# Turning the compressed queries and the softmax sums on VectorE instead of TensorE, in a hybrid encoder layer on one Trainium2 core

## The chip, the cores and the metric

The kernel runs on one core of one Trainium2 chip. Its engines work from queues of their own, each in its own order: TensorE (PE in the profile; PEld is its weight load), VectorE (DVE), ScalarE (ACT), GpSimd (POOL) and SyncE (SP), which does no arithmetic here and issues nearly all DMAs. An engine waits on semaphores that other engines or landed DMAs raise; while the instruction at the head of a queue waits, everything behind it in that queue waits too. The metric is the device time of one execution in microseconds (us); lower is better.

## The reference, cut to what matters

One layer projects x (2048 x 1024) into two groups of heads, runs gated linear attention (GLA) on the one and latent attention (MLA) on the other, and projects their concatenated outputs back, with a residual and a LayerNorm. All of it is float32. What the change touches is in the MLA branch (the compressed queries `c_q`, 256 wide, and the sums of the softmax) and in the final LayerNorm's reciprocal square root:

```python
def mla_branch(c_q, c_kv, k_rope, gate, positions, q_norm_g, w_uq, kv_norm_g, w_ukv):
    q = (rms_norm(c_q, q_norm_g) @ w_uq).reshape(B, S, MLA_HEADS, MLA_D_NOPE + MLA_D_ROPE)
    ...
    def attend(blk):
        qn, qr = blk
        s = (jnp.einsum('bqhd,bkhd->bhqk', qn, k_nope, preferred_element_type=jnp.float32)
             + jnp.einsum('bqhr,bkr->bhqk', qr, k_r, preferred_element_type=jnp.float32))
        p = jax.nn.softmax(s, axis=-1)
        return jnp.einsum('bhqk,bkhv->bqhv', p.astype(v.dtype), v)
    ...
    return o * jax.nn.silu(gate)

# at the end of the layer
x = layer_norm(DEEPNORM_ALPHA * x + mixed, ln_g[layer], ln_b[layer])
```

## The kernel before

Matrix products keep float32 accuracy by splitting each operand into a high part (`hi`, a rounding copy, on ScalarE unless said otherwise) and a low part (`lo`, operand minus high part, on VectorE or GpSimd) and multiplying three times. The sequence is cut into 16 chunks of 128 positions. There are four stages.

- **First sweep** (`sweep_a`, up to about 340 us): backward over the chunks, the GLA projections and the backward state.
- **Second sweep** (`sweep_c`, about 345 to 580 us): forward over the chunks, two chunks a step, eight steps (0 to 7). Chunk c is number j = c % 2 of its step. Per chunk: the projection `ipm`; its norms; the compressed queries `cq`; their transposition `cqT_h`, `cqT_l` (128 features on the partitions, two halves); the products `pqr` (rotary queries, from the transposed `cqT`) and, once per step for both chunks, `pq` (absorbed queries). Beside it runs the GLA forward state: DMA `SU` fetches a stored state update, GpSimd adds it to the state (`c_Sf2`, L1484), scales it into `SU` (`c_M`, L1493), and TensorE uses that in `Ob`. VectorE forms `og` and turns it in 32x32 blocks (`oT`); it goes to memory and is loaded back block by block later. The keys take that same way: `kvx`, `skv`, `kv_load`.
- **Attention** (about 600 to 1075 us): 16 blocks of one head by 512 queries. Per block 16 key tiles in eight pairs; scores `pS`, ScalarE copies, VectorE maxima, subtraction, exponential, splitting, product `o`. GpSimd and VectorE add the exponentials up over the key tiles into `acc`; `tsum` turns these 128 x 512 partial sums with four 128x128 transposes on TensorE, VectorE reduces them (`rcp`, L1714) and takes the reciprocal, ScalarE's queue stores it (`keep`).
- **Output projection** with residual and LayerNorm (to the end), whose reciprocal square root is `rsqrt_b` (L437 to L440) on a 128x1 column.

In the second sweep and in attention the order on every engine is a hand-written table: each helper `c_<name>` or step has a place (PLACE_C, PLACE_C_FIRST for step 0, PLACE_C_LAST for step 7, PLACE), in units of steps, or of tile pairs in attention; all are sorted by place, and `in_order` ties each engine to that order. A place sets order alone, not time.

In a step before the change, for each chunk, TensorE turns `cq` with two 128x128 transposes into PSUM (`c_tm`, L1407), ScalarE copies that into the high part (`c_cqTh`), VectorE subtracts for the low part (`c_cqTl`), and TensorE's `pqr` reads both: L418 and L419 the high part, L420 the low one. In TensorE's order `pqr` of a step's second chunk (j = 1) stands in the next step, among its gate products `pz`.

Of the kernel before, what the change touches and what calls it, by code (L numbers as in the profile page):

```python
# [18 lines left out]
P = 128  # L19
# [4 lines left out]
H = 4  # L24
# [68 lines left out]
    rmax=1.27,  # L93
    bmax=1.48,
    tot=11.2,
    tsum=12.04,
    rcp=13.55,
    keep=14.21,
    oh=12.34,
# [34 lines left out]
SETUP_C = ("lset", "u15", "u14", "wS", "wH", "wL", "pb0", "wa0", "wh0", "wl0", "pb1", "wa1", "wh1", "wl1")  # L134
STEP_C = ("gm1", "gm2", "gm3", "gm4", "sgm", "pq", "qah", "qal", "sqa")
CHUNK_C = ("lx", "xh", "xl", "lS", "lq", "lo", "lu", "sqm", "ssm", "rml", "rmd", "cq", "ckv", "krf", "krfa",
    "krsh", "krsl", "vh", "vl", "kvx", "tm", "cqTh", "cqTl", "ckvTh", "ckvTl", "krT", "pqr", "qrf", "qrfa",
    "tq", "qrTh", "qrTl", "Sf1", "Sf2", "M", "Ob", "oib", "sqO",
    "ss", "rgl", "rgd", "og", "oT", "soT")

FETCH_C = ("lx", "xh", "xl")
LAST_C = ("ckvTh", "ckvTl", "krT")
KV_LOADS = tuple((2 * s - 4, 2 * s - 2, float(s)) for s in range(2, NCH // 2)) + ((12, 14, 8.27),)


PLACE_C = dict(
    skv=1.6,
    kvx=(1.12, 1.44),
    ipa=(-0.08, 0.695),
    ipb=(-0.014, 0.701),  # L150
    ipc=(0.026, 0.723),
# [3 lines left out]
    pqr=(0.849, 1.355),  # L155
    tq=(1.13, 1.56),
    xh=(-0.19, -0.054),
    sqO=(0.272, 0.988),
    rgl=(0.283, 1.029),
    sqm=(0.14, 0.858),  # L160
    rml=(0.352, 0.993),
# [132 lines left out]
    sqO=(0.15, 0.435),  # L294
    rgl=(0.229, 0.457),
    sqm=(0.101, 0.657),
    rml=(0.162, 0.878),
    cq=(0.463, 1.041),
    ckv=(0.35, 1.075),
    vh=(0.865, 1.252),  # L300
# [7 lines left out]
    ss=(0.166, 0.454),  # L308
    rgd=(0.332, 0.461),
    og=(0.336, 0.508),  # L310
    ssm=(0.103, 0.733),
    rmd=(0.254, 1.022),
    krf=(0.139, 0.6),
    cqTl=(0.598, 1.211),
    ckvTl=(0.88, 1.703),
# [37 lines left out]
class K:  # L353
# [80 lines left out]

    def rsqrt_b(self, u, y, t, w, r):
        nc = self.nc
        nc.vector.tensor_tensor(t, y, u, ALU.mult)  # L437
        nc.vector.tensor_tensor(w, t, y, ALU.mult)
        nc.vector.tensor_scalar(t, w, -0.5, 1.5, ALU.mult, ALU.add)
        nc.vector.tensor_tensor(r, t, y, ALU.mult)  # L440
        return r
# [58 lines left out]
    def run(self):  # L500
        tc, nc, ins = self.tc, self.nc, self.ins
        with ExitStack() as top:
            cp = top.enter_context(tc.tile_pool(name="const", bufs=1))
            self.cp = cp
            dp = top.enter_context(tc.tile_pool(name="scr", bufs=1, space=DRAM))
            self.qd_s = [dp.tile([P, H * P], F32, name=f"qd_s{c}") for c in range(NCH)]
            self.oi_s = [dp.tile([P, H * P], F32, name=f"oi_s{c}") for c in range(NCH)]
            self.su_s = [dp.tile([P, H * P], F32, name=f"su_s{c}") for c in range(NCH)]
            self.u_s = [dp.tile([P, H * P], F32, name=f"u_s{c}") for c in range(NCH)]
            self.qa_s = [[dp.tile([P, H, QB], F32, name=f"q{p}_s{b}") for p in "hl"] for b in range(NQB)]  # L510
            self.qr_s = [dp.tile([2, QB // P, P, 256], F32, name=f"qr_s{b}") for b in range(NQB)]
# [39 lines left out]
            self.sweep_c()  # L551
            bcs.close()
            psum.close()
            self.wof = top.enter_context(tc.tile_pool(name="wof", bufs=PRE_W, side="right", reuse_waits="tile"))
            self.attention()
# [589 lines left out]
    def sweep_c(self):  # L1145


        with ExitStack() as ctx:
# [8 lines left out]

            def put(n, st, fn, *a, j=None):
                last = st == len(steps) - 1
                p = PLACE_C[n]  # L1160
                p = (last and PLACE_C_LAST.get(n)) or (not st and PLACE_C_FIRST.get(n)) or p
                todo.append((st + (p if j is None else p[j]), len(todo), fn, a))

# [11 lines left out]
            for d in chunks:  # L1175
                for n in range(4):
                    put("ip" + "abcd"[n], d["st"], self.c_ip, d, n, j=d["j"])
                for n in CHUNK_C:
                    late = d["st"] == len(steps) - 1
                    if n in (LAST_C if not late else ("kvx",)):  # L1180
                        continue
                    if (d["st"] or n not in FETCH_C) and (d["c"] < NCH - 1 or n not in ("Sf1", "Sf2")):
                        put(n, d["st"], getattr(self, "c_" + n), d, j=d["j"])
# [46 lines left out]

    def scale_w(self, ct):
        if ct:
            self.wabs = self.w1.tile([P, 2, H, P], F32, tag="qrT", name="wabs", bufs=2)
        wa = self.wabs[:, ct]
        self.nc.vector.scalar_tensor_tensor(wa, self.wa[ct], self.gq[:, ct:ct + 1],
                                            self.gkv_b[:, None, :].to_broadcast([P, H, P]), ALU.mult, ALU.mult)
# [160 lines left out]
    def kv_load(self, cs):  # L1397
        for r, src in self.blocks_of(self.kv_s[cs].rearrange("c i p (m t) -> (c i) p m t", t=32)):
            self.nc.sync.dma_start(self.kvT[r, cs].rearrange("p c i (b t) -> p (c i b) t", t=32).bitcast(F32), src)

    def c_tm(self, d):
        tp = d["tm"] = self.tr.tile([P, 4, P], F32, tag="tr", name=f"tm{d['c']}")
        src = (d["cq"][:, 0:P], d["cq"][:, P:2 * P])
# [3 lines left out]
            self.nc.tensor.transpose(tp[:, i], e, self.ident)  # L1407

    def c_cqTh(self, d):
        s = d["step"]  # L1410
        if "cqT_h" not in s:
            for p in "hl":
                s[f"cqT_{p}"] = self.w1.tile([P, 2, 2, P], F32R, tag=f"cqT_{p}", name=f"cqT_{p}{d['st']}")
        self.hi(s["cqT_h"][:, :, d["j"]], d["tm"][:, 0:2])

    def c_cqTl(self, d):
        s, j = d["step"], d["j"]
# [30 lines left out]
    def c_qrTh(self, d):  # L1448
        s = d["step"]
        if "qrT" not in s:  # L1450
            s["qrT"] = self.w1.tile([P, 2, 2, 256], F32R, tag="qrT", name=f"qrT{d['st']}", bufs=2)
        self.hi(s["qrT"][:, d["j"], 0], d["tq"])

    def c_qrTl(self, d):
# [120 lines left out]
    def attention(self):  # L1575
# [4 lines left out]
        with ExitStack() as ctx:  # L1580
# [117 lines left out]
            def close(i, shape, name, other):  # L1698
# [2 lines left out]
                p, tag = other if i == nb - 1 else (pX, "x")  # L1701
                return p.tile(shape, F32, tag=tag, name=name)

            def tsum(i):
                d = stt[i]
                d["x"] = close(i, [P, 4, P], f"sx{i}", (pA, "ap"))
                for e in range(4):
                    nc.tensor.transpose(d["x"][:, e], d["as"][:, 0, e * P:(e + 1) * P], self.ident)

            def rcp(i):  # L1710

                d = stt[i]
                rc = bs.tile([P, 4], F32, tag="rc", name=f"rc{i}")
                V.tensor_reduce(rc, d["x"], AX.X, ALU.add)  # L1714
                V.reciprocal(rc, rc)
                d["rc"] = rc

            def keep(i):
                h, b = blocks[i]
                Ac.dma_start(self.r_s[b][:, h].rearrange("o (e p) -> p (o e)", p=P), stt[i]["rc"])  # L1720

            def turn(i):

# [55 lines left out]
            put(0.5, nc.sync.dma_start, wv, self.ins["wv"])  # L1779
            put(8.6, wv_hi)  # L1780
            put(9.9, self.lo, wv_l, wv, wv_h, "pool")
            own = (("tot", tot), ("tsum", tsum), ("rcp", rcp), ("keep", keep), ("oh", oh), ("ol", ol), ("y", y), ("yc", yc))
            own_late = tuple(e for e in own if e[1] is not keep)
            for i in range(nb):
                for j in range(NP):
                    t = NP * i + j
# [311 lines left out]
```

## Time and profile before

| what | value |
|---|---|
| median of 3 runs | 1267.62 us (1267.16 to 1270.45) |
| the profiled execution | 1266.33 us; its span, first to last instruction, 1264.5 us |
| busy over the span | PE 98%, PEld 87%, DVE 72%, ACT 57%, POOL 57% |
| second sweep, one step (437.5 to 465.0 us) | PE 27.50 of 27.50 us, DVE 17.52, ACT 13.72, POOL 15.17; DMA engines 81% |
| attention (600 to 1100 us) | PE 498.38 of 500 us, DVE 423.76, ACT 409.81, POOL 446.67 |

A row of a timeline gives start, duration, engine, line of the program, operation, output<-inputs and shape; in square brackets the engine's idle time before it and who ended it. "xN" is a run of N of them merged. SPq, ACTq mark a queue's DMA issue, not the transfer. Starts are counted from the first instruction. Matmul durations overlap: what one costs on PE is the distance between starts. In the groups of one tile or line, three numbers with slashes are the least, the median and the most, in ns, and for "DMA to landing" in us from issue to landing.

### The profile page before, as it was taken

The page shows a single profiled execution, that of the slowest core. Times are in us where ns is not written, and L with a number is a line of the kernel's source. Part 1 is how long each engine was busy: PE and PEld are TensorE (multiplying, and loading weights), DVE is VectorE, ACT ScalarE, POOL GpSimd, SP SyncE. Part 2 cuts the span into 40 slices and gives each one's busy share as a digit, 9 for nine tenths or more (in the row PEclk, how much of TensorE's full clock was granted, in tenths as well). Part 3 has the DMA queues.
Part 4 walks back from the last instruction along what each step waited for, and adds up shares of the span by engine and source line. Part 5 has one row for each costly group of instructions (what it writes and reads, how often), then busy time and mean ns, then how long its engine had stood idle before and what let it go on. Part 6 is the DMA issues. An engine that isn't in the chain of part 4 may idle for free.

```text
span 1264.5 us, 19632 instructions
## 1 busy us (share of the span) xinstructions
PE 1242.3 (98%) x6890; PEld 1094.2 (87%) x6890; DVE 906.0 (72%) x1654; ACT 725.8 (57%) x1149; POOL 721.7 (57%) x443
## 2 busy tenths in 40 slices
PE   8999999999999999999999999999999999999997
PEld 7999999999899999988788888888888888887886
DVE  6635555554565666575988888888888888379998
ACT  7543443444664545445788888788888888411110
POOL 0132323223364555421798888889999999935441
PEclk9999999999999999999999999999999999999999
DMA  8224655556757788868422222202244120477773
GB/s 294 79 81 123 139 143 139 144 135 159 268 179 212 227 244 239 240 183 195 73 37 48 41 43 43 59 9 59 59 94 92 41 43 26 125 205 199 206 199 116
DMA packets 284338, 165.61 MB, mean 131 GB/s; under 512 B 185574, under 2 KB 241774, under 8 KB 284240
## 3 DMA queue, kind: packets, MB, share of 16 engines
q1 hardware_dynamic: 276176, 162.23, 48.2%
q0 software_dynamic: 672, 2.10, 0.4%
q8 instruction: 55, 0.90, 0.4%
q10 hardware_dynamic: 7392, 0.03, 0.3%
q14 instruction: 43, 0.35, 0.1%
HBM read 105.54 MB, written 58.75 MB: 130 GB/s over the span
## 4 chain that ended last, share of the span: by engine, by line
PE 86%; DVE 5%; DMA 3%; issue 2%; SPq 2%; ACT 1%; POOL 1%; DVEq 0%; POOLq 0%; ACTq 0%
PE pz L1266 7%; PE ipm L1335 5%; PE o L418 5%; PE o L419 5%; PE o L420 5%; PE pS L1599 4%; PE pS L1600 4%; PE pS L1602 4%; PE pS L1601 4%; PE pS L1603 4%; PE ipa L418 4%; PE ipa L420 4%; PE ipa L419 4%; PE ipg L420 2%; PE ipg L418 2%; PE ipg L419 2%
## 5 line engine op out<-in xcount | busy, mean ns | idle before, releaser
L370 POOL TENSOR_TENSOR pl<-s,ph 128x1024 fp32r<-128x1024 f32 x128 | 306.6, 2412 | 51.5 <-ACT ph L364 40.9
L1621 DVE TENSOR_TENSOR rm<-pS,rm 128x512 f32<-128x512 f32 x210 | 144.8, 690 | 36.3 <-ACT s L1608 30.7
L1608 ACT ACTIVATE s<-pS 128x1024 f32<-128x1024 f32 x128 | 131.3, 1025 | 60.4 <-PE pS L1603 50.0
L1645 DVE TENSOR_TENSOR s<-s,mb 128x1024 f32<-128x1024 f32 x128 | 151.2, 1213 | 8.9 <-PE mb L1639 8.8
L364 ACT ACTIVATE ph<-s 128x1024 fp32r<-128x1024 f32 x128 | 135.0, 1057 | 16.7 <-PE o L420 16.1
L1649 ACT ACTIVATE s<-s 128x1024 f32<-128x1024 f32 x128 | 131.4, 1049 | 9.4 <-DVE s L1645 9.3
L418 PE MATMUL ipa<-wah,xah 128*128 128x384 f32 (+1 forms) x384 | 128.8, 335 | 5.4 <-ACT wah L364 5.4
L419 PE MATMUL ipa<-wal,xah 128*128 128x384 f32 (+1 forms) x384 | 124.6, 324 | 0.0
L420 PE MATMUL ipa<-wah,xal 128*128 128x384 f32 (+1 forms) x384 | 124.4, 324 | 0.0
L1085 POOL TENSOR_TENSOR Sb<-Sb,Us 64x512 f32<-64x512 f32 x15 | 19.9, 1325 | 170.1 <-DVE Us L1077 161.0
L1599 PE MATMUL pS<-qh,kvT 128*128 128x512 f32 x256 | 102.4, 400 | 0.8 <-DVE rm L1621 0.4
L418 PE MATMUL o<-ph,vh 128*128 128x512 f32 x256 | 101.0, 395 | 0.0
L1600 PE MATMUL pS<-ql,kvT 128*128 128x512 f32 x256 | 99.9, 390 | 0.0
L1602 PE MATMUL pS<-rh,kvT 128*128 128x512 f32 x256 | 99.9, 390 | 0.0
L1601 PE MATMUL pS<-qh,kvT 128*128 128x512 f32 x256 | 99.8, 390 | 0.0
L1603 PE MATMUL pS<-rl,kvT 128*128 128x512 f32 x256 | 99.7, 390 | 0.0
L420 PE MATMUL o<-ph,vl 128*128 128x512 f32 x256 | 99.7, 389 | 0.0
L419 PE MATMUL o<-pl,vh 128*128 128x512 f32 x256 | 99.6, 389 | 0.0
L1672 DVE TENSOR_TENSOR ap<-ap,s 128x512 f32<-128x512 f32 x120 | 83.1, 693 | 2.7 <-ACT s L1649 0.8
L370 POOL TENSOR_TENSOR ol<-of,oh 128x512 fp32r<-128x512 f32 x32 | 43.7, 1365 | 67.8 <-ACT oh L364 62.5
L418 PEld LDWEIGHTS ipa<-wah,xah 128*128 128x128 f32 x384 | 73.1, 190 | 8.3 <-ACT wah L364 5.4
L419 PEld LDWEIGHTS ipa<-wal,xah 128*128 128x128 f32 x384 | 73.1, 190 | 1.0 <-DVE wal L370 0.5
(303 smaller groups left out, 3416.1 us busy)
## 6 DMA issues: line engine op xcount, KB each, us to landing
xcf<-xT_dram SPq DMA_DIRECT2D x16, 512.0 KB, 5.7
xr<-x_dram SPq DMA_DIRECT2D x16, 512.0 KB, 5.9
out_dram<-rr SPq DMA_DIRECT2D x32, 256.0 KB, 2.1
xaf<-xT_dram SPq DMA_DIRECT2D x14, 512.0 KB, 4.1
oib<-oi_s SPq DMA_DIRECT2D x16, 256.0 KB, 4.9
qdb<-qd_s SPq DMA_DIRECT2D x16, 256.0 KB, 3.7
SU<-su_s SPq DMA_DIRECT2D x16, 256.0 KB, 4.8
ub<-u_s SPq DMA_DIRECT2D x16, 256.0 KB, 4.5
```

The costliest lines, as they stand in the source:

```text
L364: return nc.scalar.activation(dst, src, AF.Copy).ins
L370: return e.tensor_tensor(dst, src, hi.bitcast(F32), ALU.subtract).ins
L418: mm(out, ah, bh, start=start, stop=False)
L419: mm(out, ah, bl, start=False, stop=False)
L420: mm(out, al, bh, start=False, stop=stop)
L1599: mm(ps[:, e], kh, qh, start=True, stop=False)
L1600: mm(ps[:, e], kh, ql, start=False, stop=False)
L1601: mm(ps[:, e], kl, qh, start=False, stop=False)
L1602: mm(ps[:, e], kr, rh, start=False, stop=False)
L1603: mm(ps[:, e], kr, rl, start=False, stop=True)
L1621: V.tensor_tensor(d["rm"], src[:, e], d["rm"], ALU.max)
L1645: V.tensor_tensor(s, s, d["mb"][:, None, :].to_broadcast([P, 2, QB]), ALU.subtract)
```

## The change

Three things are exchanged, and places moved to suit.

1. **Compressed queries, steps 1 to 5 (chunks 2 to 11).** The two TensorE transposes per chunk go. VectorE turns `cq` in 32x32 blocks (`c_cqx`), SyncE stores that to memory (`c_scq`) and loads it back in four DMAs that put the blocks in place (`c_lcq`), ScalarE takes the high part from what was loaded (`c_cqMh`), and GpSimd, no longer VectorE, the low part (`c_cqMl`). Steps 0, 6 and 7 keep the old way.
2. **Sums of the softmax, blocks 0 to 13.** VectorE turns `acc` in 32x32 blocks and reduces each block's rows (`tpart`), which leaves 128 x 16; TensorE turns that with one transpose instead of four; VectorE reduces 16 x 128 to 16 x 32. The reciprocals are stored in rows of 32 rather than single elements.
3. **The LayerNorm's reciprocal square root** multiplies by a per-partition scalar (`tensor_scalar`, two factors at once) in place of `tensor_tensor`: three instructions instead of four.

`qrT` now has one buffer rather than two. The diff, cut:

```diff
@@ places
-    tsum=12.04,
+    tpart=11.25,
+    tsum=12.44,
+MID_C = ("cqx", "scq", "lcq", "cqMh", "cqMl")
+PLACE_C_MID = dict(
+    ...
+    lcq=(0.64, 1.22),
+    ...
+    cqMl=(0.765, 1.345),
+    ...
-    kvx=(1.12, 1.44),
+    kvx=(1.3, 1.44),
-    sqO=(0.272, 0.988),
+    sqO=(0.272, 0.94),
@@ rsqrt_b
+        if u.shape[1] == 1:
+            nc.vector.tensor_scalar(t, y, u, y, ALU.mult, ALU.mult)
+            nc.vector.tensor_scalar(t, t, -0.5, 1.5, ALU.mult, ALU.add)
+            nc.vector.tensor_scalar(r, t, y, None, ALU.mult)
+            return r
@@ second sweep
+                    if n in (("tm", "cqTh", "cqTl") if 0 < d["st"] < len(steps) - 2 else MID_C):
+                        continue
+    def c_cqx(self, d):
+        d["cqx"] = self.w1.tile([P, 2, P], F32, tag="cqx", name=f"cqx{d['c']}", bufs=2)
+        self.nc.vector.transpose(d["cqx"].rearrange("p i f -> p (i f)"), d["cq"])
+    def c_scq(self, d):
+        self.nc.sync.dma_start(self.cq_s[d["c"]].rearrange("i p f -> p i f"), d["cqx"])
+    def c_lcq(self, d):
+        d["cqf"] = self.w1.tile([P, 2, P], F32, tag="cqf", name=f"cqf{d['c']}", bufs=2)
+        for r, src in self.blocks_of(self.cq_s[d["c"]].rearrange("i p (m t) -> i p m t", t=32)):
+            self.nc.sync.dma_start(d["cqf"][r].rearrange("p i (b t) -> p (i b) t", t=32), src)
+    def c_cqMh(self, d):
+        self.hi(self.cqT(d["step"])[0][:, :, d["j"]], d["cqf"])
+    def c_cqMl(self, d):
+        h, l = self.cqT(d["step"])
+        self.lo(l[:, :, d["j"]], d["cqf"], h[:, :, d["j"]], "pool")
@@ attention
+            def tpart(i):
+                d = stt[i]
+                V.transpose(d["as"][:, 1], d["as"][:, 0])
+                d["s16"] = bs.tile([P, QB // 32], F32, tag="s16", name=f"s16_{i}")
+                V.tensor_reduce(d["s16"], d["as"][:, 1].rearrange("p (b k) -> p b k", k=32), AX.X, ALU.add)
             def tsum(i):
                 d = stt[i]
+                if i < nb - 2:
+                    d["x"] = pX.tile([P, 4, P], F32, tag="x", name=f"sx{i}")[0:QB // 32, 0]
+                    nc.tensor.transpose(d["x"], d["s16"], self.ident)
+                    return
```

SyncE's queue around the end of step 3, before. A digit behind a name is the chunk (in `gm_s1`, `qr_s1` the block of queries): `SU9` is the state update for chunk 9.

```order
L1461 DMA ub8_5450<-u_s8_116 128x512
L1532 DMA oa_s6_147<-oT6_5181 128x4x128
L1287 DMA gm_s1_137<-gm3_5377 512x1x256
L1461 DMA SU9_5508<-su_s9_101 128x512
L1461 DMA oib9_5562<-oi_s9_85 128x512
```

The same place in SyncE's queue after:

```order
L1504 DMA ub8_5476<-u_s8_116 128x512
L1428 DMA cq_s_141<-cqx7_5484 128x2x128
L1575 DMA oa_s6_148<-oT6_5195 128x4x128
L1309 DMA gm_s1_137<-gm3_5377 512x1x256
L1433 DMA cqf7_5513<-cq_s_141 32x8x32 x4
L1504 DMA SU9_5534<-su_s9_101 128x512
L1504 DMA oib9_5586<-oi_s9_85 128x512
```

The store of chunk 7's turned queries and the four loads that read it back have come ahead of the fetch of `SU9`.

GpSimd's queue at the same place, before; `Sf9` is the state, `krf8`, `krs8`, `qrf7` belong to the rotary parts:

```order
L1369 TENSOR_TENSOR krf8_5486<-krf8_5486,rope1_8_5487 128x64
L1484 TENSOR_TENSOR Sf9_5484<-Sf9_5484,SU9_5508 64x512
L1493 TENSOR_TENSOR SU9_5508<-Sf8_5193,cw_216 64x512
L1480 TENSOR_TENSOR Sf10_5584<-Sf9_5484,cw_216 64x512
L370 TENSOR_TENSOR krs8_5629<-krf8_5486,krs8_5629 128x64
```

GpSimd's queue there after:

```order
L1391 TENSOR_TENSOR krf8_5507<-krf8_5507,rope1_8_5508 128x64
L1527 TENSOR_TENSOR Sf9_5505<-Sf9_5505,SU9_5534 64x512
L1536 TENSOR_TENSOR SU9_5534<-Sf8_5202,cw_217 64x512
L384 TENSOR_TENSOR cqT_l3_5365<-cqf7_5513,cqT_h3_5364 128x2x128
L1523 TENSOR_TENSOR Sf10_5603<-Sf9_5505,cw_217 64x512
```

The low part of chunk 7's queries (`cqT_l3`, step 3's tile) has moved from VectorE to GpSimd, behind the two instructions that need `SU9`.

ScalarE's queue a little later, before, where chunk 8's high part is made and the next x is split (`xch`):

```order
L1362 ACTIVATE ckv8_5639<-ipm8_5387,rm8_r_5552 128x128
L1358 ACTIVATE cq8_5641<-ipm8_5387,rm8_r_5552 128x256
L364 ACTIVATE qrT3_5482<-qrx7_5695 128x256
L364 ACTIVATE cqT_h4_5703<-tm8_5668 128x2x128
L364 ACTIVATE vh_3893<-ckv8_5639 128x128
L364 ACTIVATE xch_3717<-xcf10_5586 128x8x128
L1271 ACTIVATE gm4_5742<-pz4_5494 128x1024
```

ScalarE's queue there after:

```order
L378 ACTIVATE qah3_5685<-pq3_5638 128x1024
L378 ACTIVATE qrT3_5503<-qrx7_5726 128x256
L378 ACTIVATE vh_3894<-ckv8_5668 128x128
L378 ACTIVATE cqT_h4_5765<-cqf8_5738 128x2x128
L378 ACTIVATE xch_3718<-xcf10_5612 128x8x128
L1293 ACTIVATE gm4_5778<-pz4_5520 128x1024
```

The high part now reads what the loads bring (`cqf8`), not PSUM (`tm8`), and still stands ahead of `xch` and the gate's exponentials `gm4`; `ckv8` and `cq8` have come ahead of `qah3`.

On SyncE the loads of `cqf8` stand behind `ql_s` and `ub9`, where before the load of x (`xcf11`) followed `ub9` directly. On VectorE the turn `cqx7` stands between `og7` and `oT7`. TensorE's order is as before but for the transposes that are gone.

More of the change, by code (lines that the diff above doesn't have):

```diff
@@ L136 @@
 CHUNK_C = ("lx", "xh", "xl", "lS", "lq", "lo", "lu", "sqm", "ssm", "rml", "rmd", "cq", "ckv", "krf", "krfa",
-    "krsh", "krsl", "vh", "vl", "kvx", "tm", "cqTh", "cqTl", "ckvTh", "ckvTl", "krT", "pqr", "qrf", "qrfa",
+    "krsh", "krsl", "vh", "vl", "kvx", "cqx", "scq", "lcq", "cqMh", "cqMl", "tm", "cqTh", "cqTl", "ckvTh", "ckvTl", "krT", "pqr", "qrf", "qrfa",
     "tq", "qrTh", "qrTl", "Sf1", "Sf2", "M", "Ob", "oib", "sqO",
@@ L141 @@
 FETCH_C = ("lx", "xh", "xl")
+MID_C = ("cqx", "scq", "lcq", "cqMh", "cqMl")
+PLACE_C_MID = dict(
+    cqx=(0.535, 1.1025),
+    scq=(0.54, 1.105),
+    lcq=(0.64, 1.22),
+    cqMh=(0.76, 1.34),
+    cqMl=(0.765, 1.345),
+    pqr=(0.849, 1.42),
+    qrf=(0.853, 1.465),
+    qrfa=(0.95, 1.485),
+    pq=1.47,
+    qah=1.53,
+)
 LAST_C = ("ckvTh", "ckvTl", "krT")
@@ L296 @@
     sqm=(0.101, 0.657),
-    rml=(0.162, 0.878),
+    rml=(0.187, 0.878),
     cq=(0.463, 1.041),
@@ L310 @@
     og=(0.336, 0.508),
-    ssm=(0.103, 0.733),
-    rmd=(0.254, 1.022),
+    ssm=(0.1025, 0.733),
+    rmd=(0.29, 1.022),
     krf=(0.139, 0.6),
@@ L513, in run @@
             self.kv_s = dp.tile([NCH, 3, P, P], F32, name="kv_s")
+            self.cq_s = dp.tile([NCH, 2, P, P], F32, name="cq_s")
             self.oa_s = [dp.tile([H, P, P], F32, name=f"oa_s{c}") for c in range(NCH)]
@@ L1159, in put @@
                 last = st == len(steps) - 1
-                p = PLACE_C[n]
+                p = (0 < st < len(steps) - 2 and PLACE_C_MID.get(n)) or PLACE_C.get(n)
                 p = (last and PLACE_C_LAST.get(n)) or (not st and PLACE_C_FIRST.get(n)) or p
@@ L1232, in scale_w @@
         if ct:
-            self.wabs = self.w1.tile([P, 2, H, P], F32, tag="qrT", name="wabs", bufs=2)
+            self.wabs = self.w1.tile([P, 2, H, P], F32, tag="qrT", name="wabs")
         wa = self.wabs[:, ct]
@@ L1399, in kv_load, with cqT @@
             self.nc.sync.dma_start(self.kvT[r, cs].rearrange("p c i (b t) -> p (c i b) t", t=32).bitcast(F32), src)
+    def c_cqx(self, d):
[7 more added lines that the diff above has]
+            self.nc.sync.dma_start(d["cqf"][r].rearrange("p i (b t) -> p (i b) t", t=32), src)
+    def cqT(self, s):
+        if "cqT_h" not in s:
+            for p in "hl":
+                s[f"cqT_{p}"] = self.w1.tile([P, 2, 2, P], F32R, tag=f"cqT_{p}", name=f"cqT_{p}{s['st']}")
+        return s["cqT_h"], s["cqT_l"]
+    def c_cqMh(self, d):
[3 more added lines that the diff above has]
+        self.lo(l[:, :, d["j"]], d["cqf"], h[:, :, d["j"]], "pool")
     def c_tm(self, d):
@@ L1409, in c_cqTh @@
     def c_cqTh(self, d):
[L1410 to L1414, printed above, removed]
+        self.hi(self.cqT(d["step"])[0][:, :, d["j"]], d["tm"][:, 0:2])
     def c_cqTl(self, d):
@@ L1450, in c_qrTh @@
         if "qrT" not in s:
-            s["qrT"] = self.w1.tile([P, 2, 2, 256], F32R, tag="qrT", name=f"qrT{d['st']}", bufs=2)
+            s["qrT"] = self.w1.tile([P, 2, 2, 256], F32R, tag="qrT", name=f"qrT{d['st']}")
         self.hi(s["qrT"][:, d["j"], 0], d["tq"])
@@ L1712, in rcp @@
                 d = stt[i]
-                rc = bs.tile([P, 4], F32, tag="rc", name=f"rc{i}")
+                if i < nb - 2:
+                    rc = d["rc"] = bs.tile([QB // 32, 32], F32, tag="rc", name=f"rc{i}")
+                    V.tensor_reduce(rc, d["x"].rearrange("b (k q) -> b q k", k=4), AX.X, ALU.add)
+                    V.reciprocal(rc, rc)
+                    return
+                rc = bs.tile([P, 4], F32, tag="rc4", name=f"rc{i}")
                 V.tensor_reduce(rc, d["x"], AX.X, ALU.add)
@@ L1719, in keep @@
                 h, b = blocks[i]
-                Ac.dma_start(self.r_s[b][:, h].rearrange("o (e p) -> p (o e)", p=P), stt[i]["rc"])
+                Ac.dma_start(self.r_s[b][:, h].rearrange("o (e q) -> (o e) q", q=32), stt[i]["rc"])
             def turn(i):
@@ L1781, in attention @@
             put(9.9, self.lo, wv_l, wv, wv_h, "pool")
-            own = (("tot", tot), ("tsum", tsum), ("rcp", rcp), ("keep", keep), ("oh", oh), ("ol", ol), ("y", y), ("yc", yc))
-            own_late = tuple(e for e in own if e[1] is not keep)
+            own = (("tot", tot), ("tpart", tpart), ("tsum", tsum), ("rcp", rcp), ("keep", keep), ("oh", oh), ("ol", ol), ("y", y), ("yc", yc))
+            own_late = tuple(e for e in own if e[1] not in (keep, tpart))
             for i in range(nb):
```

## The prediction

> **What bounds the kernel now.** I read the page's busy times first, then the busy time by stretches, then one step of the second sweep engine by engine.
>
> ```profile
> PE 1242.3 (98%) x6890; PEld 1094.2 (87%) x6890; DVE 906.0 (72%) x1654; ACT 725.8 (57%) x1149; POOL 721.7 (57%) x443
> ```
>
> ```profile
> 437.50:465.00 27.50, 27.50 (x201) 26.81 (x200) 17.52 (x63) 13.72 (x36) 15.17 (x16) 1.00 0.81 231
> 548.00:576.00 28.00, 25.21 (x180) 23.79 (x180) 18.71 (x70) 10.35 (x38) 6.04 (x9) 0.94 0.65 183
> 600.00:1100.00 500.00, 498.38 (x2285) 411.48 (x2285) 423.76 (x562) 409.81 (x441) 446.67 (x194) 1.00 0.27 55
> ```
>
> PE never rests in a middle step (27.50 of 27.50 us), nor in attention (498.38 of 500). So work taken from PE shortens the kernel, and any new wait of PE lengthens it by its whole length. The profiled execution took 1266.3 us, 1.3 under the median 1267.6; I add 1.3 to the sum.
>
> **The PE work removed.** What a transpose costs is the distance between starts:
>
> ```profile
> 639.71 0.39 PE L1603 MATMUL pS<-rl,kvT 128*128 128x512 f32 x1
> 639.94 0.60 PE L1708 MATMUL sx<-ident,acc 128*128 128x128 f32 x4
> ...
> 640.61 0.40 PE L1600 MATMUL pS<-ql,kvT 128*128 128x512 f32 x1
> ```
>
> ```profile
> 1144.33 0.39 PE L420 MATMUL po<-woh,ol 128*128 128x512 f32 x1
> 1144.56 0.27 PE L1726 MATMUL rt<-ident,rc 128*4 128x128 f32 x1
> ...
> 1144.90 0.40 PE L419 MATMUL pmb<-wol,oh 128*128 128x512 f32 x1
> ```
>
> ```profile
> 449.32 0.29 PE L1266 MATMUL pz<-xch,wzl 128*128 128x256 f32 x1
> 449.44 0.38 PE L1407 MATMUL tm<-ident,cq 128*128 128x128 f32 x2
> ...
> 449.78 0.28 PE L1266 MATMUL pz<-xcl,wzh 128*128 128x256 f32 x1
> ```
>
> With four transposes between them, a product and the next but one start 0.90 us apart; with a single narrow one, as `tsum` will be, 0.57. That saves 0.33 a block, times 14 blocks: 4.6 us. The pair for the queries stretches 0.24 (two starts 0.12 apart) to 0.46: 0.22 a chunk, 2.2 us for ten, if PE does not wait there anyway.
>
> VectorE pays in attention:
>
> ```profile
> L1529 DVE STREAM_TRANSPOSE oT<-og x16: 711/712/715, 367.8 to 562.6; 128x512 f32<-128x512 f32 x16
> L1621 DVE TENSOR_TENSOR rm<-pS,rm 128x512 f32<-128x512 f32 x210 | 144.8, 690 | 36.3 <-ACT s L1608 30.7
> ```
>
> `tpart` adds a turn and a reduction of 128x512; at 0.71 each, as the turn `oT` of that size, 1.4 us a block, and the later reduction shrinks. The maxima alone sit idle 36.3 us over 16 blocks, 2.3 each, waiting for ScalarE's copies; that covers 1.4. I cost it at nothing; without the cover it is at most 14 x 1.4 = 19.6 us.
>
> In the output projection `rsqrt_b` gets cheaper:
>
> ```profile
> L437 DVE TENSOR_TENSOR ln_t<-ln_y,u x16: 129/1242/1293, 1124.0 to 1259.2; 128x1 f32<-128x1 f32 x16
> L439 DVE TENSOR_SCALAR ln_t<-ln_t x16: 130/154/155, 1126.3 to 1259.6; 128x1 f32<-128x1 f32 x16
> ```
>
> ```profile
> PE pmb L420 <- POOL ol L370: 0.7, 1, 0.7
> PE rt L1726 <- ACT rt L1732: 0.7, 1, 0.7
> ```
>
> A `tensor_tensor` on a 128x1 column takes 1.24 us, a `tensor_scalar` 0.15, so VectorE is relieved of some us a chunk. But PE waits only twice there, 0.7 us each, and of the last chunk's chain one instruction of about 0.2 goes. Between 0.2 and 1.6 I take 0.5 us. The Trainium skill (GPSIMD Engine Reference, Specifications) says that GpSimd shares its SBUF interface with VectorE, in contention with VectorE instructions that read two SBUF inputs; by that rule all the slow ones would become quick, both PE waits could end, and this term would be 1.6 instead of 0.5.
>
> **The new way of the queries, second chunk of a step.** Chunk 7, before:
>
> ```profile
> 463.29 1.13 DVE L1523 SCALAR_TENSOR_TENSOR og<-Ob,rg_r,ub 128x128 f32<-128x128 f32 x4
> 464.58 0.66 SPq L1461 DMA_DIRECT2D SU<-su_s  x1
> 465.66 0.40 DVE L1446 STREAM_TRANSPOSE qrx<-qrf 128x256 f32<-128x256 f32 x1
> ```
>
> ```profile
> 468.46 0.42 DVE L370 TENSOR_TENSOR cqT_l<-tm,cqT_h 128x256 fp32r<-128x256 f32 x1
> ```
>
> ```profile
> 469.50 0.28 PE L420 MATMUL pqr<-wqr_h,cqT_l 128*128 128x256 f32 x1
> ```
>
> ```profile
> 470.59 1.29 POOL L1484 TENSOR_TENSOR Sf<-Sf,SU 64x512 f32<-64x512 f32 x1 [2.88 <-DMA SU<-su_s]
> 471.95 1.03 POOL L1493 TENSOR_TENSOR SU<-Sf,cw 64x512 f32<-64x512 f32 x1
> 474.34 0.73 POOL L1442 TENSOR_TENSOR qrf<-qrf,rope 128x256 f32<-128x256 f32 x1
> ```
>
> The low part was ready at 468.88 and PE read it at 469.50: 0.6 us to spare. Now the low part stands on GpSimd behind `Sf` and `SU`, which wait for the fetch of `SU9`; even unmoved, these end at 472.98, after PE wants the operand. And the fetch is moved too: it stands on SyncE behind the four loads, and these behind the landing of the store. Prices of the transfers:
>
> ```profile
> su_s<-Us SPq DMA_DIRECT2D x14, 128.0 KB, 2.3
> kv_s<-kvx SPq DMA_DIRECT2D x7, 384.0 KB, 3.2
> qdb<-qd_s SPq DMA_DIRECT2D x16, 256.0 KB, 3.7
> ```
>
> ```profile
> L1399 SPq DMA_DIRECT2D kvT<-kv_s x28: 425/524/1553, 402.3 to 577.4; - x28
> DMA to landing us min/median/max: 2.7/3.4/4.0
> ```
>
> ```profile
> DMA to landing us min/median/max: 2.6/4.8/5.9
> ```
>
> The last row is of `SU`, the one above it of `kvT` and `kv_s`. Step by step: `og` ends at 464.42, `cqx` (as `qrx`, 0.40) at 464.85, the store goes out at 464.95 and lands 2.3 later (128 KB, as `su_s`): 467.25. Four issues of 0.52: 469.35. `SU9` lands 3.15 later (midway between its own least, 2.6, and the 3.7 of an equal load, since the queue has drained by then): 472.5. `Sf` and `SU` with their gaps take 2.49, `cqT_l` as a 128x256 GpSimd instruction 0.78 with its gap, the semaphore 0.1: 475.87 for 469.50, 6.4 us late. With the low prices (0.425 an issue, 2.6 for `SU9`) it is 5.4, with the dear ones (3.2 for the store, as `kv_s`, and 4.8) 8.9. The queries' own loads land earlier than this. Queued behind the waiting `pqr` is all of PE's work. The Trainium skill (DMA: Bandwidth & Descriptors, Anatomy of one DMA) gives about 2.0 us fixed plus bytes at 436 GB/s for a DMA, written down for the GpSimd path. By that rule, an estimate, the store takes 2.3 and `SU9` 2.6, and the whole forecast falls by 5 x 0.55 = 2.8 us; the rows above agree only at their lower ends, as this stage's queue is loaded.
>
> **The first chunk of a step.** PE reads its queries late, so the wait shows elsewhere:
>
> ```profile
> 449.65 0.98 SPq L1461 DMA_DIRECT2D ub<-u_s  x1
> ```
>
> ```profile
> 449.86 0.38 ACT L364 ACTIVATE cqT_h<-tm 128x256 fp32r<-128x256 f32 x1 [1.15 <-PE tm L1407]
> 452.73 1.06 ACT L364 ACTIVATE xch<-xcf 128x1024 fp32r<-128x1024 f32 x1 [2.28 <-PE pz L1266]
> ```
>
> ```profile
> 456.92 1.23 DVE L1280 TENSOR_TENSOR gm<-pz,gm 128x1024 f32<-128x1024 f32 x1 [6.22 <-ACT gm L1277]
> ```
>
> The four loads start at 450.7, behind `ub`; the last goes out at 452.26 and lands 3.4 later (the median of `kvT`), 455.66. `cqT_h` then ends at 456.1, and `xch`, which ran at 452.73, is 3.4 us late (2.4 with issues of 0.425 and 2.7, 4.0 with 4.0). Behind it on ScalarE are the gate's exponentials, VectorE waits for these (6.22 us idle already), and behind `gm` on VectorE stand the norms of the next second chunk, so its `cq` and `cqx` come 3.4 later too. This adds to the 6.4.
>
> **The clock.** Two waits for `pqr`, in step 6, show what a stop costs afterwards:
>
> ```profile
> 553.67 0.58 PE L420 MATMUL pqr<-wqr_h,cqT_l 128*128 128x256 f32 x1 [1.15 <-DVE cqT_l L370]
> ...
> 554.70 0.57 PE L1335 MATMUL ipm<-wmh,xch 128*128 128x448 f32 x1
> 555.07 0.57 PE L1335 MATMUL ipm<-wml,xch 128*128 128x448 f32 x1
> ```
>
> The `ipm` products start 0.37 us apart, and the granted clock of that stretch is 0.94: 28 x 0.06 = 1.7 us lost. `pq` and what hangs on it (`qah`, its stores, then the loads of `cqf`) run at that pace, so each longer stop costs 1.7 more (none if the clock holds).
>
> **The sum.** Five steps at 6.4 + 3.4 + 1.7 = 11.5: +57.5. The 2.2 us of PE transposes in these steps only lengthen the waits and count nothing. Attention -4.6, tail -0.5. In all +52.4: 1266.3 + 52.4 + 1.3 = 1320. With the low prices and no clock loss 5 x 7.8 - 5.1 = +33.9: 1302; with the high ones 5 x 14.6 - 5.1 = +67.9: 1336. Costed at nothing besides: the bytes (0.5 MB a step beside 231 GB/s x 27.5 us = 6.4 MB; the DMA engines' share of 0.81 has room, the more so in longer steps); `qrT`'s second buffer (its stores go out in the step that writes it, the next writes follow a step later, and a late one would hold ScalarE, at most by one landing of 2 to 5 us a step); the moved `kvx` (its store is read back a step later) and `sqO` (some 0.3 us either way on ScalarE ahead of `cq`). The tables of before and after differ in nothing else that PE waits for.
>
> **The rivals.**
> - *The round trip is hidden and only PE's saving shows*: -4.6 - 2.2 - 0.5 = -7.3, 1260. For it speaks PE's 98%; against it the 0.6 us to spare and the two queues. It decides for faster only if `SU9` lands some 6 us earlier than its place allows. Chance 0.05, 0.01 of it within 0.3%.
> - *Only GpSimd's order counts*, the transfers being quick or the delays swallowing each other: low part at 472.98 + 0.88 = 473.86, 4.4 us late; 5 x 4.4 - 5.1 = +16.9, 1285. Between it and the forecast's low end lie mixtures. Chance 0.13.
> - *VectorE becomes the bound of attention too*: up to 19.6 us on top, 1340, or transfers dearer than assumed. Against: the idle 2.3 us a block. Chance 0.07.
> - The forecast, slower by the waits for the queries: 0.75.
>
> The range 1290 to 1336 leaves out the first rival, half of the second and most of the third, less than 0.2. A difference under 0.3% (3.8 us) can't be told from none: faster 0.05, same 0.01, slower 0.94.
>
> **What would show it.** Right: PE's waits list `pqr` L434 (the line of L420 then) behind POOL five times, each over 5 us; PE's share in steps 1 to 5 falls to some 70% and a step takes about 39 us instead of 27.7; the clock dips after each; `gm` starts later in its step. In attention a block is 0.33 us shorter. Wrong: `pqr` waits for nothing, or `SU9` lands before 470 on the old count, or PE waits in attention for VectorE's maxima.

## The result and the profile after

| | before | after |
|---|---|---|
| median | 1267.62 us (5 runs, 1265.96 to 1270.45) | 1319.16 us (5 runs, 1317.89 to 1321.23) |
| ratio | | 1.0404 (95% interval 1.0388 to 1.0420) |
| span of the profiled execution | 1264.5 us | 1319.0 us |

The busy times on the page after; PE, at 98% before, now rests:

```profile
PE 1257.7 (95%) x6828; PEld 1106.3 (84%) x6828; DVE 894.8 (68%) x1666; ACT 728.3 (55%) x1149; POOL 733.3 (56%) x453
```

What PE waited for, after (us in total, times, longest us):

```profile
PE pqr L434 <- POOL cqT_l L384: 17.5, 6, 4.6
PE pz L1288 <- DVE og L1566: 16.5, 6, 3.6
PE pqr L432 <- ACT cqT_h L378: 8.2, 5, 2.4
PE ipa L432 <- ACT wah L378: 5.5, 1, 5.5
```

The first three are new or grown, five or six times each, 42.2 us in all; before, `pz` waited 1.2 us, `pqr` 1.4 for ScalarE and never for GpSimd. The last, in the first sweep, was there before. Two whole steps after, from a step's first `pz` to the next one's (columns as in the prediction's stretches: length, busy time of PE, PEld, DVE, ACT, POOL, granted clock, DMA share, GB/s), and attention:

```profile
450.86:491.48 40.62, 32.53 (x197) 31.05 (x197) 17.28 (x63) 13.68 (x36) 16.36 (x19) 0.87 0.64 175
491.48:532.00 40.52, 31.89 (x197) 30.63 (x197) 17.27 (x63) 13.68 (x36) 16.38 (x19) 0.87 0.64 176
700.00:1116.00 416.00, 416.00 (x1890) 342.56 (x1888) 378.21 (x516) 354.57 (x378) 378.24 (x164) 1.00 0.23 51
```

A step of 27.7 us has become one of 40.6, PE is busy for 80% of it, and the clock averages 0.87. Attention still has no gap. In the second of these stretches PE reads the queries of chunk 7, the second chunk of its step. Engine by engine, in order of time:

```profile
491.25 0.43 DVE L1425 STREAM_TRANSPOSE cqx<-cq 128x256 f32<-128x256 f32 x1
491.71 0.38 SPq L1428 DMA_DIRECT2D cq_s<-cqx  x1
495.21 1.98 SPq L1433 DMA_DIRECT2D cqf<-cq_s  x4
497.23 0.45 SPq L1504 DMA_DIRECT2D SU<-su_s  x1
499.49 0.42 ACT L378 ACTIVATE cqT_h<-cqf 128x256 fp32r<-128x256 f32 x1 [3.97 <-DMA cqf<-cq_s]
499.96 0.39 PE L432 MATMUL pqr<-wqr_h,cqT_h 128*128 128x256 f32 x1 [2.44 <-ACT cqT_h L378]
500.46 1.26 POOL L1527 TENSOR_TENSOR Sf<-Sf,SU 64x512 f32<-64x512 f32 x1 [6.21 <-DMA SU<-su_s]
501.79 1.03 POOL L1536 TENSOR_TENSOR SU<-Sf,cw 64x512 f32<-64x512 f32 x1
502.79 0.71 POOL L384 TENSOR_TENSOR cqT_l<-cqf,cqT_h 128x256 fp32r<-128x256 f32 x1
503.56 0.58 PE L434 MATMUL pqr<-wqr_h,cqT_l 128*128 128x256 f32 x1 [3.10 <-POOL cqT_l L384]
```

This is the chain the prediction laid out: store, landing, four issues, fetch of `SU`, `Sf`, `SU`, low part, PE. PE stops twice: 2.44 us for the high part, which needs only the queries' own loads, and 3.10 more for the low part behind `SU`. Before, the low part was read 4.63 us after the step's first `pz` (469.50 against 464.87); here it is 12.08 us (503.56 against 491.48). The first chunk of the next step (8), in the same trace:

```profile
519.86 0.42 ACT L378 ACTIVATE cqT_h<-cqf 128x256 fp32r<-128x256 f32 x1 [7.34 <-DMA cqf<-cq_s]
520.18 1.04 ACT L378 ACTIVATE xch<-xcf 128x1024 fp32r<-128x1024 f32 x1
521.13 1.01 ACT L1293 ACTIVATE gm<-pz 128x1024 f32<-128x1024 f32 x1
524.36 1.23 DVE L1302 TENSOR_TENSOR gm<-pz,gm 128x1024 f32<-128x1024 f32 x1 [10.76 <-ACT gm L1299]
530.73 1.13 DVE L1566 SCALAR_TENSOR_TENSOR og<-Ob,rg_r,ub 128x128 f32<-128x128 f32 x4
532.00 0.36 PE L1288 MATMUL pz<-xch,wzh 128*128 128x256 f32 x1 [3.09 <-DVE og L1566]
```

The late high part holds ScalarE, so `xch` and the gate are late, VectorE makes `og` late, and PE's next `pz`, which takes over the PSUM buffer that `og` reads (`pz`, `pq` and `Ob` rotate through one tag), stands for 3.09 us.

### The profile page after: what moved, and what is told of

It is laid out like the page before. It is cut to its first block, busy times and chain, and to the rows that moved or that the text cites. A ratio compares the mean times of both kernels' runs of the same rounds, so it can differ in the third digit from the quotient of the medians.

```text
span 1319.0 us, 19621 instructions
## 1 busy us (share of the span) xinstructions
PE 1257.7 (95%) x6828; PEld 1106.3 (84%) x6828; DVE 894.8 (68%) x1666; ACT 728.3 (55%) x1149; POOL 733.3 (56%) x453
## 4 chain that ended last, share of the span: by engine, by line
PE 75%; DMA 7%; DVE 5%; ACT 4%; issue 3%; SPq 3%; POOL 3%; DVEq 0%; POOLq 0%; ACTq 0%
PE o L432 4%; PE o L433 4%; PE o L434 4%; PE pS L1642 4%; PE pS L1644 4%; PE pS L1643 4%; PE pS L1645 4%; PE pS L1646 4%; PE ipa L432 4%; PE ipa L434 4%; PE ipa L433 4%; PE pz L1288 3%; PE ipg L434 2%; PE ipg L432 2%; PE ipg L433 2%
## 5 line engine op out<-in xcount | busy, mean ns | idle before, releaser
L1664 DVE TENSOR_TENSOR rm<-pS,rm 128x512 f32<-128x512 f32 x210 | 144.6, 688 | 18.3 <-ACT s L1651 12.7
L378 ACT ACTIVATE ph<-s 128x1024 fp32r<-128x1024 f32 x128 | 135.0, 1056 | 16.5 <-PE o L434 15.9
L434 PE MATMUL ipa<-wah,xal 128*128 128x384 f32 (+1 forms) x384 | 124.5, 324 | 0.0
L434 PE MATMUL o<-ph,vl 128*128 128x512 f32 x256 | 99.8, 390 | 0.0
L1288 PE MATMUL pz<-xch,wzh 128*128 128x256 f32 x256 | 79.4, 312 | 16.5 <-DVE og L1566 16.5
L1288 PE MATMUL pz<-xch,wzl 128*128 128x256 f32 x256 | 78.0, 306 | 0.0
```

The source lines that it names most:

```text
L434: mm(out, al, bh, start=False, stop=stop)
L1288: self.nc.tensor.matmul(s["pz"][:, h], self.Wz[k][w][:, h * P:(h + 1) * P], x2(x, k), start=(k == 0 and p == 0), stop=stop.get(h) == (k, p))
L1664: V.tensor_tensor(d["rm"], src[:, e], d["rm"], ALU.max)
```

## The experiments

**The round trip taken out again, the rest kept.** Every chunk goes by PE transposes.

```diff
-                p = (0 < st < len(steps) - 2 and PLACE_C_MID.get(n)) or PLACE_C.get(n)
+                p = PLACE_C.get(n)
-                    if n in (("tm", "cqTh", "cqTl") if 0 < d["st"] < len(steps) - 2 else MID_C):
+                    if n in MID_C:
```

> The queries go by PE transposes again in every chunk; the attention sums, the short reciprocal root, qrT's single buffer and the moved places stay. Theory (the round trip makes all of the loss): 1267.6 - 4.3 (attention, as in the trace of the changed kernel) - 1.3 (tail) = 1262, and PE waits in the second sweep as before. Rival (moved places or the single buffer cost part of it): 1266 or more, with waits of PE in the second sweep that before lacks.

1260.96 us against 1267.78, ratio 0.9947 (0.9932 to 0.9962). The waits for the queries and for `og` are back to what they were:

```profile
PE pqr L434 <- DVE cqT_l L384: 1.4, 1, 1.4
PE pz L1288 <- DVE og L1566: 0.9, 1, 0.9
```

So the round trip makes all of the loss; the other parts gain 6.7 us, and `qrT`'s single buffer and the moved places cost nothing to be seen. This is the fastest kernel of the study.

**The round trip alone.** `tpart` and the short `rsqrt_b` undone.

> The attention sums by four PE transposes and the long reciprocal root again; the round trip of the queries stays. Theory (the parts add): 1319.2 + 6.8 = 1326. Rival (the short root, ahead of cq in the chain of the round trip, helped there too): 1330 or more.

1323.21 us, ratio 1.0444 (1.0428 to 1.0459). The parts add within 3 us; the short root did not help the round trip.

**The low part on VectorE.**

```diff
-    cqMl=(0.765, 1.345),
+    cqMl=(0.765, 1.3935),
-        self.lo(l[:, :, d["j"]], d["cqf"], h[:, :, d["j"]], "pool")
+        self.lo(l[:, :, d["j"]], d["cqf"], h[:, :, d["j"]])
```

> The low part is made by VectorE (behind oT), not by GpSimd behind Sf and SU. Theory (GpSimd's order, which waits for the fetch of SU, makes the second half of the pqr stop): the third pqr product follows the first within 0.6 us instead of 3.2 to 5.1, so 5 x 3.5 = 17.5 less: 1302; 1289 if PE's clock also holds after the shorter stop. Rival (only GpSimd's order counts, own loads are in time): the whole pqr stop goes, 5 x 7.2 + 5 x 2 = 46 less: 1273. Rival (the loads alone hold it): no change, 1319.

1290.16 us, ratio 1.0176 (1.0160 to 1.0192): 29.0 less than the changed kernel. PE's waits, then one chunk's products:

```profile
PE pz L1288 <- DVE og L1566: 16.5, 6, 4.1
PE pqr L432 <- ACT cqT_h L378: 6.6, 5, 2.2
```

```profile
485.67 0.39 PE L432 MATMUL pqr<-wqr_h,cqT_h 128*128 128x256 f32 x1 [0.40 <-ACT cqT_h L378]
485.89 0.28 PE L433 MATMUL pqr<-wqr_l,cqT_h 128*128 128x256 f32 x1
486.13 0.39 PE L434 MATMUL pqr<-wqr_h,cqT_l 128*128 128x256 f32 x1
```

The wait behind GpSimd is gone from the list and the third product follows the first by 0.46 us. The granted clock from 400 us to the end of this stage averages 0.95, for 0.88 in the changed kernel. The clock still drops, but less, and the time comes near the theory's case in which it holds, 1289. What stays at `pqr` is the wait for the queries' own loads, so the rival with GpSimd's order alone (1273) falls, and the rival with the loads alone (1319) too.

**The fetch of `SU` ahead of the four loads.** `lcq=(0.64, 1.22)` becomes `(0.64, 1.265)`.

> For the second chunk of a step the fetch of SU stands on SyncE ahead of the four loads of cqf, not behind. Theory (the low part waits for Sf and SU, and they for a fetch that went out 4 us late): Sf and SU are done when the high part is, the third pqr product then waits 0.8 us for the low part instead of 3.2 to 5.1, and the loads go out 0.5 us later: 5 x 2.3 = 11 less: 1308. Rival (the fetch's place does not matter, the transfers as such are slow): within 2 us of 1319. Rival (only this queue counts): the whole second stop goes, 1300 or less.

1307.75 us, ratio 1.0318 (1.0300 to 1.0337): 11.4 less, as the theory had it. The low part's wait falls from 17.5 to 6.7 us:

```profile
PE pz L1288 <- DVE og L1566: 14.6, 5, 4.1
PE pqr L432 <- ACT cqT_h L378: 9.7, 5, 2.5
PE pqr L434 <- POOL cqT_l L384: 6.7, 6, 2.0
```

The place of one DMA issue on SyncE is worth 2.3 us a step, without any transfer being faster: from issue to landing the fetches of `SU` take 3.9 us here (median), 3.2 in the changed kernel.

**The gate ahead of the first chunk's high part on ScalarE.** `cqMh=(0.76, 1.34)` and `cqMl=(0.765, 1.345)` become `(0.84, 1.34)` and `(0.842, 1.345)`.

> For the first chunk of a step the high part stands on ScalarE behind xch and the three gate passes, not ahead of them. Theory (PE's stop at the first pz of a step is the high part's wait for its loads, passed on through xch, gm and VectorE to og): these stops of 2.9 to 3.6 us go, six of them, 16 to 20 less: 1299 to 1303, the stops at pqr stay 6 to 7 us behind. Rival (that stop comes from og's own chain, or from VectorE's added cqx): no change, 1319. Rival (the half clock after that stop is lost on top): 8 less again, 1292.

1309.65 us, ratio 1.0333 (1.0317 to 1.0349): 9.5 less where 16 to 20 were expected. The stops at `pz` of 2.9 to 3.6 us are gone, as the theory says, and in the middle steps that is worth 3.0 to 4.1 us each. But the first such step has a new one:

```profile
400.62 1.02 ACT L1293 ACTIVATE gm<-pz 128x1024 f32<-128x1024 f32 x1 [4.53 <-DMA ql_s<-qal]
403.73 0.40 ACT L378 ACTIVATE cqT_h<-cqf 128x256 fp32r<-128x256 f32 x1
404.18 0.58 PE L432 MATMUL pqr<-wqr_h,cqT_h 128*128 128x256 f32 x1 [4.32 <-ACT cqT_h L378]
```

The gate's first pass waits until the store of `qal` has landed, and the high part now stands behind it. `gm` and `qal` are tiles of one tag with one buffer: a coupling that the prediction had not seen.

**The first chunk's loads earlier on SyncE instead.** `lcq=(0.58, 1.22)`: behind the store of `cqx`, ahead of the query stores.

> For the first chunk of a step the four loads of cqf stand on SyncE right behind the store of cqx, not behind the query stores and ub; ScalarE's order is as in the changed kernel. Theory (ScalarE's high part is late only because its loads go out late on this queue): PE's six stops at the first pz go, 15.4 less: 1302 to 1304, the stops at pqr stay. Rival (the landing itself is slow, or the high part's place on ScalarE delays xch whatever the loads do): no change, 1319.

1311.11 us, ratio 1.0341 (1.0324 to 1.0359): 8 less, where 15.4 were expected. **The same with the low part on VectorE:**

> The early loads of the first chunk, and the low part on VectorE. Theory (two separate chains, whose losses add): 29 + 15.4 less than the changed kernel: 1275; what is left is PE's wait for the second chunk's own loads, about 2 to 2.5 us a step, at full clock. Rival (the chains overlap, one takes over what the other frees): 1285 or more.

1296.80 us, ratio 1.0237 (1.0219 to 1.0254): worse than the low part on VectorE alone. **And with the readers later on PE**, which asks whether PE work in front hides the round trip:

```diff
-    pqr=(0.849, 1.42),
-    qrf=(0.853, 1.465),
-    qrfa=(0.95, 1.485),
-    pq=1.47,
-    qah=1.53,
+    pqr=(0.849, 1.5325),
+    qrf=(0.853, 1.534),
+    qrfa=(0.95, 1.545),
+    pq=1.533,
+    qah=1.54,
```

> As the last, and pqr and pq of a step stand on PE behind 36 (24 for pq) more pz products, 4.3 us of work, which cover the wait for the second chunk's loads. Theory (the round trip costs only where PE has nothing in front of its readers): the saving of the PE transposes shows at last, 1261 - 2.2 = 1259. Rival (the later pq makes the query stores, and through them the next step, late; or the added transfers cost by themselves): 1265 or more.

1298.03 us, ratio 1.0245 (1.0226 to 1.0264), where 1259 was expected. The three misses have a cause in common, which shows clearest in the last: no wait for the round trip at a second chunk is left, yet five steps have a stop of 5.21 us at `pz`. SyncE, ScalarE, VectorE and PE there:

```profile
502.97 0.64 SPq L1330 DMA_DIRECT2D ql_s<-qal  x1
508.34 1.03 ACT L1293 ACTIVATE gm<-pz 128x1024 f32<-128x1024 f32 x1 [4.49 <-DMA ql_s<-qal]
517.97 1.13 DVE L1566 SCALAR_TENSOR_TENSOR og<-Ob,rg_r,ub 128x128 f32<-128x128 f32 x4
519.24 0.55 PE L1288 MATMUL pz<-xch,wzh 128*128 128x256 f32 x1 [5.21 <-DVE og L1566]
```

Loads ahead of the query stores, or a later `pq`, make `ql_s` land later. The gate waited for that landing in two steps of the first of these three kernels (7.2 us), in five of the last (23.5 us), and in six of the second:

```profile
ACT gm L1293 <- DMA ql_s<-qal: 23.0, 6, 5.3
```

Then `pz` follows the gate by 10.9 us (519.24 against 508.34), as it did in the changed kernel (532.00 against 521.13) and, by 10.8, before (492.53 against 481.71). In the first of the three kernels this is not the whole miss: its stops at `pqr` also grew, from 25.7 us to 31.6. The gate stood at that landing already before, with next to no room:

```profile
481.71 1.03 ACT L1271 ACTIVATE gm<-pz 128x1024 f32<-128x1024 f32 x1 [0.26 <-DMA ql_s<-qal]
```

In the changed kernel the gate waited for it only once, 2.1 us. So the shared buffer is no part of that kernel's loss to speak of; it takes over where the loads come earlier or `pq` later.

**A buffer of its own for `qal`**, on top of the last. The diff shows the main line. To make room, `cqx`, `cqf` and `oT` have one buffer each instead of two, and the stores of `oT` (`soT`) stand earlier on SyncE.

```diff
-        s["ql"] = self.w1.tile([P, H, 256], F32R, tag="gm", name=f"qal{s['st']}")
+        s["ql"] = self.w1.tile([P, H, 256], F32R, tag="qal", name=f"qal{s['st']}")
```

> As e8_later_product, and qal no longer shares a buffer with the gate's gm (room for it: cqx, cqf and oT single, oT stored earlier). In e8 ScalarE's first gate pass started when the store of qal had landed, each step, and PE's stop at pz followed 10.9 us behind. Theory (that shared buffer is what hands the lateness of the loads on to the gate): gm starts 4 to 4.5 us earlier, the stop of 5.2 us falls to about 0.7 and the clock holds: 1263 (1259 to 1266). Rival (the gate is late because pq is late, whatever the buffer): stops of 3 us or more stay, 1285 or more.

1273.59 us, ratio 1.0056 (1.0043 to 1.0068): 24.4 less. The gate's wait for the store, 23.5 us in the kernel without this buffer, is gone from ScalarE's waits, so the shared buffer carried most of what was lost there; what the single buffers and the earlier stores add or cost was not separated. The expected 1263 is not reached:

```profile
PE pz L1288 <- DVE og L1566: 12.2, 6, 3.2
```

**The low part on VectorE and the gate first**, SyncE's queue as in the changed kernel:

> The low part on VectorE, and the high part of a step's first chunk behind the gate's passes on ScalarE; SyncE's queue as in the changed kernel, so that the query stores go out before the loads. Theory (e7 failed by its queue order, not because the two chains overlap): no stops at pz, PE's wait for the second chunk's loads of 2 to 3 us a step stays, the first step costs 3: 1274 to 1280. Rival (the chains overlap): 1285 or more.

1285.12 us, ratio 1.0149 (1.0132 to 1.0166). No stop at `pz` is left, but each second chunk still waits 2.2 to 3.2 us for its own loads, and the first step 4.05; the expectation had the shape right and 5 to 11 us too little. **The gate first, with `qal`'s own buffer and the later readers:**

> As e9_own_buffer, with the first chunk's high part on ScalarE behind xch and the gate's passes. Theory (in e9 the gate still waits some 1.6 us a step for the loads, through the high part ahead of xch): the stops of 0.8 to 3.2 us at pz shrink by 1.6 each and the clock no longer drops: 1263 to 1266. Rival (the rest is the chain from pq over og, not the loads): 1272 to 1275.

1274.93 us, ratio 1.0057 (1.0044 to 1.0070): no gain. With the loads of `cqf` no longer ahead of the gate, PE still waits 11.2 us in all for `og`. What holds `og` there stays open; the traces give two leads that no run tested. With `qal`'s own buffer alone the gate itself still starts late, 18.5 to 19.5 us after the first `pz` of the middle steps for 16.5 to 16.8 before, and ahead of it on ScalarE stands `qrT`, whose input now comes late from GpSimd (VectorE waits 18.7 us for `qrf`, 6.2 before). With the gate first ScalarE waits for the load of x instead, 8.3 us in five times, never so before.

## Why the prediction was right, step by step

1319.16 against 1320, inside the range, and the forecast's own case. From first `pz` to first `pz`, the six affected steps are longer by 1.5, 12.0, 13.0, 12.9, 10.9 and 10.0 us, 60.2 in all. Attention and tail give back 4.3 and 1.4: 54.5, by which the span grew, where the prediction summed 52.4. That the forecast comes within 1 us of the median is in part luck. The profiled execution after took 1321.23, 2.1 over its median, so the medians differ by only 51.5. The errors of the terms also cancel in part: the second chunks cost 4 us more in all than forecast, and the tail gave back 0.9 more.

- **Second chunk, 6.4 forecast: 7.2 measured.** Read off the five steps as for chunk 7 above, the third `pqr` product starts 11.0 to 13.1 us after the step's first `pz`, 11.84 on average, for 4.63. The store landed after 1.9 us in three steps and 3.5 to 3.7 in two (2.3 taken), and the fetch of `SU` went out 0.8 later than forecast. `SU`'s landing (3.2 from issue to `Sf` on average) and the GpSimd steps came as forecast. The estimate by the Trainium skill's rule (DMA: Bandwidth & Descriptors, Anatomy of one DMA), 2.3 for the store and 2.6 for `SU9`, lies over the 1.9 of three stores and under the median of `SU` here, 3.2. With the low part on VectorE the third product starts 7.7 us after `pz` on average: 3.0 of the 7.2 are the queries' own round trip, 4.2 GpSimd's order behind a moved fetch.
- **First chunk, 3.4 forecast: 3.3 measured**, the mean of the five stops at `pz`. The chain is the one named, but its end was put in the wrong place: I had it delay the next second chunk's queries; PE stops before that, at `pz`, because `pz` needs the buffer that `og` reads.
- **The clock, 1.7 forecast: about 2.1**, what is left of the four full steps (12.2 - 6.9 - 3.2). There were two half-clock spells a step, not one. The first stands ahead of the stops at `pqr` (491.93 to 495.34, for chunk 7), where slower products only shorten the wait that follows.
- **Attention, -4.6 forecast: -4.3.** The maxima's transposes, before and after, first and last start (the last two numbers with a "to"):

```profile
L1627 PE MATMUL mx<-ident,rm x64: 271/272/327, 599.8 to 1060.7; 128*128 128x128 f32 x64
L1670 PE MATMUL mx<-ident,rm x64: 270/272/327, 660.1 to 1116.6; 128*128 128x128 f32 x64
```

By the unrounded starts 460.8 against 456.5, 0.31 a block. VectorE's cover held: the maxima's idle time fell from 36.3 to 18.3 us, and PE did not wait for them. The rival with VectorE as the bound is out.

```profile
L1664 DVE TENSOR_TENSOR rm<-pS,rm 128x512 f32<-128x512 f32 x210 | 144.6, 688 | 18.3 <-ACT s L1651 12.7
```

- **Tail, -0.5 forecast: -1.4.** This term was mis-sized most in proportion, within its 0.2 to 1.6. All the slow column operations became quick, as the rows after show:

```profile
L452 DVE TENSOR_SCALAR ln_t<-ln_y,u x16: 238/268/273, 1179.0 to 1313.9; 128x1 f32<-128x1 f32 x16
L454 DVE TENSOR_SCALAR ln_r<-ln_t,ln_y x16: 197/214/216, 1180.2 to 1314.4; 128x1 f32<-128x1 f32 x16
PE pmb L434 <- POOL ol L384: 0.2, 1, 0.2
```

1.24 us became 0.27, and of PE's two waits of 0.7 there one is 0.2 and the other gone. Why the old ones were slow, the two traces show, before and after:

```profile
1160.34 1.32 POOL L370 TENSOR_TENSOR ol<-of,oh 128x512 fp32r<-128x512 f32 x1 [4.52 <-ACT oh L364]
1160.43 1.25 DVE L437 TENSOR_TENSOR ln_t<-ln_y,u 128x1 f32<-128x1 f32 x1
```

```profile
1276.33 1.33 POOL L384 TENSOR_TENSOR ol<-of,oh 128x512 fp32r<-128x512 f32 x1 [2.64 <-ACT oh L378]
1276.43 0.27 DVE L452 TENSOR_SCALAR ln_t<-ln_y,u 128x1 f32<-128x1 f32 x1
```

Before, 29 of the 48 `tensor_tensor` of this column start while a GpSimd instruction runs; 28 of them end 0.01 to 0.02 us after it, whatever is left of it then (0.17 to 1.28 us). The 19 others take 0.13 to 0.16. The `tensor_scalar` of after ends long before the GpSimd instruction beside it. The Trainium skill's rule (GPSIMD Engine Reference, Specifications), contention of GpSimd with VectorE instructions that read two SBUF inputs, had given 1.6 for this term; the traces bear it out.
- **The transposes' 2.2 us** never showed: the best kernel with the round trip (1273.6) is 12.6 us behind the one without (1261.0).
- **The sign.** The wait list has `pqr` L434 behind POOL five times, and a sixth of 0.2 us, but at 2.7 to 4.6 us, not over 5: the stop is shared with the high part ahead of it (0.8 to 2.4). Steps of about 39 us were forecast; 38.6 to 40.6 came. PE is busy for 80% of a step, not 70: at half the clock its products take longer and count as busy (`pqr` products start 0.21 us apart at 503.94, 0.12 at 480.85).

## What to carry to other kernels

An engine that never rests gains from work taken off it only if its replacement arrives in time for that engine's in-order queue. A round trip through memory must be costed with everything queued on its way: the fetch it pushes back, the instructions ahead of its consumer on the consumer's engine, and what else waits in that queue. Where stops move rather than shrink, look for a shared buffer: here one tag for `gm` and `qal` tied the gate to a store's landing.

## What the runs showed of the hardware

**The clock.** Between 60 and 1200 us all half-clock spells of these traces (a granted clock of 0.50) last 3.41 us or a multiple, and within a trace they lie on one grid. Two such stretches of the changed kernel, then four of the low part on VectorE (PE's busy time is the first number behind the length, the clock stands third from the end):

```profile
488.52:491.93 3.41, 0.45 (x4) 0.48 (x5) 2.92 (x14) 1.95 (x10) 3.41 (x3) 1.00 0.00 0
491.93:495.34 3.41, 3.41 (x19) 3.41 (x18) 3.38 (x13) 1.42 (x4) 1.12 (x3) 0.50 0.51 140
```

```profile
442.74:446.16 3.42, 1.47 (x12) 1.50 (x13) 3.28 (x15) 1.77 (x7) 2.60 (x2) 1.00 0.09 26
446.16:449.57 3.41, 3.41 (x18) 3.41 (x17) 3.24 (x14) 1.29 (x5) 0.91 (x2) 0.50 0.93 263
517.83:521.25 3.42, 1.90 (x14) 1.74 (x15) 3.28 (x14) 1.59 (x6) 0.95 (x1) 1.00 0.88 248
521.25:524.66 3.41, 3.41 (x32) 3.41 (x31) 0.81 (x4) 0.00 (x0) 3.25 (x5) 1.00 1.02 346
```

PE never rests in the half-clock stretch from 491.93, and at 495.34 full clock is back. A full-clock stretch with PE busy for 1.47 us is followed by half clock, one with 1.90 is not. Counted over the full-clock stretches between 60 and 1200 us of all thirteen traces, the 71 followed by half clock have at least 1.60 us without a product in them, the other 4167 at most 1.95; between these two both happen. So a stop of 2.2 us costs clock or not by where it falls on the grid: 2.24 us ahead of 444.69 did, 2.19 ahead of 519.35 did not (both of the low part on VectorE). The Trainium skill (TensorE: Matmul & The Clock Gate, The HAM clock gate) gives a free-running window of 3413 ns, which agrees with the 3.41 us here, and the drop after at least one idle window; here stretches that were about half idle (1.60 to 1.95 of 3.41 us) were already enough.
